# One inference step of a hybrid HGRN2 and attention layer on one core: VectorE's front tiles, the reciprocals' rings and the adaLN sums

## The chip, the core and the metric

The kernel runs on one core of one Trainium2 chip. The core has TensorE (PE, matmuls into PSUM), VectorE (DVE), ScalarE (ACT), GpSimd (POOL) and SyncE (SP, which here issues most DMAs). The engines run side by side, each through its own queue in order, and wait for each other on semaphores. The metric is the device time of one execution in microseconds, as a median over runs.

## What is computed

One trunk layer over 1024 latent tokens and 256 context tokens of width 1024, in float32:

```python
m = silu(cond) @ w_ada + b_ada                 # adaLN: 6 x 1024 columns, for c and c_ctx
sh1, sc1, g1, sh2, sc2, g2 = split(m, 6)
h = rms_norm(x, norm_mix_w) * (1.0 + sc1) + sh1
z = h @ w_in                                   # hq, hf (two directions), hi, hg, aq, ak, av, gl
o_a = attention(q, k, v)                       # 8 heads, 2 kv heads; latent: 512 cached + 1024 keys
o_h = rms_norm(hgrn(...)) * silu(hg)           # two directions, 4 heads, chunks of 32
g = sigmoid(gl)
merged = g[0] * (o_h @ w_ho) + g[1] * (o_a @ w_ao)
x = x + g1 * (merged @ w_out)
h = rms_norm(x, norm_ffn_w) * (1.0 + sc2) + sh2
x = x + g2 * (square(relu(h @ w_ff1)) @ w_ff2)
y = rms_norm(x, final_norm_w)
```

Context and latent tokens have conditioning vectors of their own, so each adaLN column is needed twice.

## The kernel before

**Numbers.** A matrix product is made of three matmuls in the format fp32r: each operand is split into a high part (rounded, written by ScalarE in `split`, L312) and a low part (the rest, a subtraction on VectorE, L313). L345, L346 and L347 are high x high, high x low and low x high in `mm3`; L362 to L364 the same with tokens as output rows.

**Tokens.** They come in three tiles, `TT`: t=0 and t=1 of 512 latent tokens, t=2 of 256 context tokens. Activations lie transposed, 128 channels by the tile's tokens, in eight chunks `kc`.

**Order.** TensorE's instructions run in the order in which the program issues them. The other engines' are put in order by the framework's scheduler ahead of time, with priorities from the program's order; `tc.high_priority` moves one up, and `tc.issue_after(x)` keeps one behind `x`. Tiles live in rings: `RINGS` gives the number of buffers of each, `RING_OF` the ring of each name. A tile that asks for a buffer waits until the last reader of an earlier tile is done. Ring X has 20 buffers, B 4, D 3, F and G 2. PSUM has two banks under the tag "t" (`ps_t`).

**The front.** The rows of x are loaded, normalised and transposed into `ps_t` (`norm1_tr`, L285). `norm1_col` then makes the modulated activation: ScalarE writes the high part `hi` from PSUM (L297); a full value `xn` is made from PSUM, by ScalarE (L302) or, for `kc` 1, 4 and 7 of t=0 and t=1, by VectorE (L300); VectorE subtracts, `lo = xn - hi` (L303). `front_z` uses both (L644, L645, L650).

**adaLN sums.** The first 16 of 48 column chunks (of 128) are made in the front. The others come in pairs of chunks, in two ways. `ada_sum` works on GpSimd: a 1024x256 block of `w_ada` is loaded into one of the two buffers of `wraw`, which the weights of `w_in` use too, multiplied by the conditioning vector and added over its eight row blocks (L197 to L204), for both vectors, into the two accumulators `ACC`. Its `late` lets TensorE add over the 128 partitions: four matmuls with the accumulator as the stationary operand and one column of ones as the moving one (L210), then VectorE adds the bias (L212). `ada_cols` does a whole pair on TensorE in four column groups (L178), evicts on ScalarE (L180), transposes (L184) and adds on VectorE.

**The filler.** While attention runs, `with_ada` yields the matmuls of ten groups of `w_in` columns (hq, hf, hf, hi, hg, twice); `Filler` feeds them in between attention's own, spread evenly. Groups of hi and hg are token-wise (`grp.tok`). In each group but the first there is one `ada_sum`: started at 0.25 of the group and finished at 0.9, in the last at 0.02 and 0.42; nine pairs in all. During the HGRN scans a second filler yields the gate logits' eight groups (`gls`), and seven pairs are made there by `ada_cols`.

**Attention's output.** `trans` transposes the exponentials into `ps_t` (L877), ScalarE and VectorE split them (L880), `value` multiplies by V (L891, L892). Sums of exponentials are turned into reciprocals and stored as rows in `RS`; outputs go to `OA`, those of HGRN to `OH`.

**The projections.** After the last gate logits, for t in the order 0, 2, 1, eight tiles `or` are loaded from `OH` (c < 4) and `OA`; for `OA` a second tile `or` of reciprocals is loaded, broadcast over 64 partitions each, and multiplied in (L1337); each is split into `oT` (L312, L313), in the buffers that `hT`, the activations of the gate logits, leave free. Then for each of eight output chunks and each t, `mm3` multiplies by `w_hgrn_out` and `w_attn_out`.

Of the kernel before, what the change touches and what calls it, by code (L numbers as in the profile page):

```python
# [11 lines left out]
AF = mybir.ActivationFunctionType  # L12
ALU = mybir.AluOpType
AX = mybir.AxisListType

P = 128
D = 1024
# [27 lines left out]
def build(ctx, tc, I, O, C):  # L45
# [15 lines left out]
    def close(*names):  # L61
        for n in names:
            open_pools.pop(n).close()
# [9 lines left out]
    def PS(tag, shape=(P, 512)):  # L73
        tag = "g" if tag == "p" else tag
        return ps.tile(list(shape), F32, tag=tag, name="ps_" + tag, bufs=PSB[tag])

    def S(shape=(P, 512), dt=F32, name=None, ring=None):
        ring = ring or RING_OF[name]
        return (xb if ring == "X" else sb if ring in "DE" else sl).tile(list(shape), dt, tag="s" + ring, name=name, bufs=RINGS[ring])
# [20 lines left out]
    def dma(out, in_):  # L100
        return sp.dma_start(out=f32(out), in_=f32(in_))
# [4 lines left out]
    def f32(ap):  # L106
        return ap.bitcast(F32)
# [85 lines left out]
    def ada_sum(ci, acc):  # L193

        raw = wraw(I["w_ada"], KC, ci * P)
        w = [ada_l[:, :, c:c + 1].broadcast_to([P, KC, 256]) for c in range(2)]
        g_.tensor_tensor(acc[0], raw[:, 0], w[0][:, 0], op=ALU.mult)  # L197
        for k in range(1, KC):
            g_.tensor_tensor(acc[1], raw[:, k], w[0][:, k], op=ALU.mult)
            g_.tensor_tensor(acc[0], acc[0], acc[1], op=ALU.add)  # L200
        g_.tensor_tensor(raw, raw, w[1], op=ALU.mult)
        for n in (4, 2):
            g_.tensor_tensor(raw[:, 0:n], raw[:, 0:n], raw[:, n:2 * n], op=ALU.add)
        g_.tensor_tensor(acc[1], raw[:, 0], raw[:, 1], op=ALU.add)  # L204

        def late():
            pt = PS("t")
            for b in range(2):
                for c in range(2):
                    pe.matmul(pt[:, 2 * c + b:2 * c + b + 1], acc[c][:, b * P:(b + 1) * P], ones, start=True, stop=True)  # L210
            with tc.high_priority(offset=600):
                v.tensor_tensor(modc[:, :, ci:ci + 2], pt[:, 0:4].rearrange("p (c b) -> p c b", c=2),  # L212
                                cols[:, B_ADA + ci:B_ADA + ci + 2].unsqueeze(1).broadcast_to([P, 2, 2]), op=ALU.add)
        return late


# [21 lines left out]
    def hpair(t):  # L238
        n = TT[t][1]
        if n == 512:  # L240
            return H(t), H(t)
        x = h_first.pop() if h_first else H(2)
        return x[:, 0, :], x[:, 1, :]
# [44 lines left out]
    def norm1_col(t, kc, pt, blocks=None):  # L288
        t0, n, cond = TT[t]
        if not blocks or blocks[0] == 0:  # L290
            hT[t][kc] = hpair(t)
        c = slice(blocks[0] * P, blocks[-1] * P + P) if blocks else slice(0, n)
        hi, lo = [x[:, c] for x in hT[t][kc]]
        pt, xn = pt[:, c], xnb[:, kc % 4, c]
        sc, sh = s1[:, cond, kc:kc + 1], modc[:, cond, kc:kc + 1]
        with tc.high_priority(offset=600):
            made = s_.activation(hi, pt, AF.Identity, scale=sc, bias=sh)  # L297

            if kc % 3 == 1 and t < 2:
                v.tensor_scalar(xn, pt, sc, sh, op0=ALU.mult, op1=ALU.add)  # L300
            else:
                s_.activation(xn, pt, AF.Identity, scale=sc, bias=sh)  # L302
            low[0] = v.tensor_tensor(lo, xn, f32(hi), op=ALU.subtract)  # L303
        return made

    low = [None]
# [938 lines left out]
    def zh(c):  # L1245
        return (Group(HQ + 256 * c, hq_consume(c), False), Group(HF + 256 * c, hf_consume(0, c), False),
                Group(HF + 512 + 256 * c, hf_consume(1, c), False), Group(HI + 256 * c, hi_consume(c), True),
                Group(HG + 256 * c, hg_consume(c), True))
# [3 lines left out]
    def with_ada(groups, ahead, behind):  # L1252

        late = []
        for i, grp in enumerate(groups):
            nxt = groups[i + 1] if i + 1 < len(groups) else None
            at, acts = 0.0, []
            if i and ahead:
                ci = ahead.pop(0)
                t0, t1 = (0.25, 0.9) if nxt else (0.02, 0.42)  # L1260
                acts = [(t0, lambda: late.append(ada_sum(ci, ACC))), (t1, lambda: late.pop()())]
            for need, n, gen in grp.stages():
                if not grp.tok and need == (0,):
                    jobs = [(0.5, lambda: grp.part(1))]
                elif nxt:
                    jobs = [(0.05, nxt.load), (0.5, lambda: nxt.part(0))]
                    if nxt.tok and not grp.tok:
                        jobs.append((0.75, lambda: nxt.part(1)))
                else:
                    jobs = []  # L1270
                for j, x in enumerate(gen):
                    if 0 in need and j == 6 and todo:
                        todo.pop()()
                    while jobs and j >= jobs[0][0] * n:
                        jobs.pop(0)[1]()
                    at += x
                    while acts and at >= acts[0][0] * 26.2:
                        acts.pop(0)[1]()
                    yield x
            if behind:  # L1280
                ci = behind.pop(0)
                todo.append(ada_cols(PS("g"), wraw(I["w_ada"], KC, ci * P), ci))
                yield 1.8
        if todo:
            todo.pop()()

    fz = Filler(with_ada([*zh(0), *zh(1)], list(range(16, 34, 2)), []), 250.0)
    while pending:
        fz.add(1.0)
        flush(1.0)  # L1290
# [4 lines left out]
    gls = [Group(GL + 256 * c, gl_consume(c), False) for c in range(8)]  # L1295
    with tc.high_priority(offset=600):
        gls[0].part(0)
    fg = Filler(with_ada(gls, [], list(range(34, 48, 2))), 196.0)
    hgrn(fg, fz.rest)
    fg.rest()  # L1300
    close("sl")
    wo1 = pool("wo1")

# [17 lines left out]
        return GR[r:r + 8, :].rearrange("(o a) b -> o (a b)", o=1).broadcast_to([P, D])  # L1321


    MT = (0, 2, 1)
    oT = [[None] * 8 for _ in range(3)]
    for t in MT:
        n = TT[t][1]
        for c in range(8):
            r = S(name="or")
            dma(r[:, 0:n], (OH if c < 4 else OA)[c % 4][t])  # L1330
            if c >= 4:
                q = S(name="or")
                for i in range(2):
                    r0 = 10 * (2 * (c - 4) + i) + TT[t][0] // P
                    row = RS[r0:r0 + n // P, :].rearrange("(o b) p -> o (b p)", o=1)
                    dma(q[64 * i:64 * i + 64, 0:n], row.broadcast_to([64, n]))
                v.tensor_tensor(r[:, 0:n], r[:, 0:n], q[:, 0:n], op=ALU.mult)  # L1337
            oT[t][c] = hpair(t)
            split(oT[t][c][0], oT[t][c][1], r[:, 0:n])
    mg = [[None] * KC for _ in range(3)]  # L1340
    WO = [[None] * 4 for _ in range(2)]

# [674 lines left out]
```

## Time and profile before

| what | value |
|---|---|
| median of 3 runs | 2041.67 us (2040.69 to 2041.69) |
| the profiled execution | 2040.07 us |
| its span, first to last instruction | 2038.3 us |
| mean granted TensorE clock | 0.999 |
| front, then the first products of attention | to about 131 us |
| attention, with the first filler | about 131 to 700 us |
| HGRN, with the second filler | about 700 to 1001 us |
| rest of the gate logits, then projections | to 1015 us, then from 1015 us |

The profile is one execution. A page gives the busy time of each engine, the chain of work that ended last and the costliest groups of instructions; further views give the instructions in order of time, the waits (who waited for whom) and the busy time of stretches. A line such as L313 can be a helper's and stand for many tiles: the names of the tiles (out<-in) tell them apart.

### The profile page before, as it was taken

The numbers are of one execution on the slowest core, as the hardware profiler recorded it, in microseconds if no ns is written. First come the engines' busy times: TensorE is split into PE (matmuls) and PEld (weight loads), VectorE is DVE, ScalarE is ACT, GpSimd is POOL, SyncE is SP. The second block draws the span as 40 slices with busy tenths as digits, with TensorE's granted clock in tenths as the row PEclk, the third lists the DMA queues.
The fourth block names the chain that finished last, engine by engine and source line by source line (L and its number), as shares of the span: only waits on it lengthen the run. The fifth ranks groups of instructions, "written<-read, shape, count | busy, mean of one in ns | idle before, by whom it ended". The sixth has DMA issues, their size and how long they took to land.

```text
span 2038.3 us, 33049 instructions
## 1 busy us (share of the span) xinstructions
PE 2004.0 (98%) x12246; PEld 1734.4 (85%) x12246; DVE 1346.3 (66%) x2474; ACT 940.0 (46%) x1965; POOL 526.7 (26%) x594
## 2 busy tenths in 40 slices
PE   7899999999999999999999999999999999999998
PEld 5698889988889988888878889988888888888886
DVE  5865665655665789877355635886666666577786
ACT  4635555555565423323312335755545544333443
POOL 1471321433303655544022101222112200000120
PEclk9999999999999999999999999999999999999999
DMA  9452211322122455554844424854454489455764
GB/s 317 155 193 83 81 58 47 105 93 76 38 92 80 149 158 175 160 176 149 249 145 143 170 104 148 258 183 146 146 164 145 147 309 357 135 166 171 237 236 138
DMA packets 222626, 320.00 MB, mean 157 GB/s; under 512 B 19161, under 2 KB 140801, under 8 KB 222465
## 3 DMA queue, kind: packets, MB, share of 16 engines
q1 hardware_dynamic: 209984, 277.99, 42.8%
q0 software_dynamic: 12480, 39.91, 5.3%
q8 instruction: 96, 1.57, 0.3%
q14 instruction: 66, 0.53, 0.1%
HBM read 232.05 MB, written 85.78 MB: 156 GB/s over the span
## 4 chain that ended last, share of the span: by engine, by line
PE 90%; DMA 4%; DVE 3%; ACT 1%; issue 1%; SPq 0%; POOL 0%; POOLq 0%; DVEq 0%; ACTq 0%
PE ps_g L345 8%; PE ps_g L346 7%; PE ps_g L347 7%; PE ps_s L845 4%; PE ps_t L877 4%; PE ps_g L362 2%; PE ps_g L892 2%; PE ps_g L364 2%; PE ps_g L363 2%; PE ps_g L1804 2%; PE ps_g L1806 2%; PE ps_g L1805 2%; PE ps_g L891 2%; PE ps_s L1649 2%; PE ps_s L1651 2%; PE ps_s L1650 2%
## 5 line engine op out<-in xcount | busy, mean ns | idle before, releaser
L345 PE MATMUL ps_g<-hs,wsp 128*128 128x512 f32 (+1 forms) x896 | 322.6, 360 | 0.0
L346 PE MATMUL ps_g<-hs,wsp 128*128 128x512 f32 (+1 forms) x896 | 309.2, 345 | 2.9 <-DVE hs L313 2.9
L347 PE MATMUL ps_g<-hs,wsp 128*128 128x512 f32 (+1 forms) x896 | 309.3, 345 | 0.0
L312 ACT ACTIVATE wsp<-wraw 128x512 fp32r<-128x512 f32 (+1 forms) x186 | 116.7, 668 | 208.4 <-PE ps_g L346 81.2
L846 DVE TENSOR_REDUCE mx<-ps_s 128x1 f32<-128x512 f32 (+1 forms) x208 | 138.1, 668 | 112.6 <-PE ps_s L845 110.6
L880 DVE TENSOR_TENSOR pTl<-ps_t,pTh 128x512 fp32r<-128x512 f32 x200 | 136.4, 684 | 88.0 <-ACT pTh L880 87.6
L313 DVE TENSOR_TENSOR wsp<-wraw,wsp 128x512 fp32r<-128x512 f32 (+1 forms) x186 | 147.4, 817 | 70.0 <-ACT wsp L312 69.7
L347 PEld LDWEIGHTS ps_g<-hs,wsp 128*128 128x128 f32 x896 | 169.3, 189 | 21.7
L345 PEld LDWEIGHTS ps_g<-hs,wsp 128*128 128x128 f32 x896 | 169.6, 189 | 20.3 <-issue 4.4
L346 PEld LDWEIGHTS ps_g<-hs,wsp 128*128 128x128 f32 x896 | 169.9, 190 | 18.2 <-DVE hs L313 3.4
L880 ACT ACTIVATE pTh<-ps_t 128x512 fp32r<-128x512 f32 x200 | 118.2, 602 | 139.3 <-PE ps_t L877 137.6
L312 ACT ACTIVATE ah<-ar 128x640 fp32r<-128x640 f32 (+1 forms) x112 | 80.9, 723 | 185.9 <-PE ps_g L1805 102.3
L857 ACT ACTIVATE pexp<-ps_s,ngm 128x512 f32<-128x512 f32 (+1 forms) x208 | 137.4, 669 | 42.7 <-DVE ngm L850 42.3
L313 DVE TENSOR_TENSOR ah<-ar,ah 128x640 fp32r<-128x640 f32 (+1 forms) x112 | 92.0, 822 | 78.2 <-ACT ah L312 77.8
L845 PE MATMUL ps_s<-Kl,Ql 128*128 128x512 f32 (+1 forms) x416 | 129.5, 411 | 0.0
L877 PE MATMUL ps_t<-ident,pexp 128*128 128x128 f32 x800 | 120.0, 272 | 0.1
L362 PE MATMUL ps_g<-wsp,hs 128*128 128x256 f32 x400 | 115.8, 289 | 0.0
L364 PE MATMUL ps_g<-wsp,hs 128*128 128x256 f32 x400 | 112.9, 282 | 0.0
L363 PE MATMUL ps_g<-wsp,hs 128*128 128x256 f32 x400 | 112.6, 281 | 0.0
L892 PE MATMUL ps_g<-pTl,Vl 128*128 128x256 f32 x400 | 104.2, 283 | 0.2
L891 PE MATMUL ps_g<-pTh,Vl 128*128 128x256 f32 x400 | 104.0, 281 | 0.0
L877 PEld LDWEIGHTS ps_t<-ident,pexp 128*128 128x128 f32 x800 | 94.4, 140 | 9.5 <-issue 0.6
(436 smaller groups left out, 5363.0 us busy)
## 6 DMA issues: line engine op xcount, KB each, us to landing
ar<-AF SPq DMA_DIRECT2D x112, 320.0 KB, 3.3
wraw<-in_w_ff SPq DMA_DIRECT2D x32, 1024.0 KB, 6.4
wr<-in_w_ff SPq DMA_DIRECT2D x128, 256.0 KB, 4.4
wraw<-in_w_in SPq DMA_DIRECT2D x18, 1024.0 KB, 5.6
wraw<-in_w_ada SPq DMA_DIRECT2D x16, 1024.0 KB, 5.4
AF<-a POOLq DMA_DIRECT2D x48, 256.0 KB, 2.7
AF<-t POOLq DMA_DIRECT2D x48, 256.0 KB, 2.3
wa<-in_w_ada SPq DMA_DIRECT2D x32, 256.0 KB, 5.9
```

The source lines that it names most:

```text
L312: s_.activation(hi, raw, AF.Copy)
L313: return v.tensor_tensor(lo, raw, f32(hi), op=ALU.subtract)
L345: pe.matmul(out, hi[:, k, :], mh, start=(first and k == 0), stop=False)
L346: pe.matmul(out, hi[:, k, :], ml, start=False, stop=False)
L347: pe.matmul(out, lo[:, k, :], mh, start=False, stop=(last and k == kcs - 1))
L362: pe.matmul(po[:, bb, :], mh[:, off:off + P], wh[:, k % 4, :], start=(k == 0), stop=False)
L363: pe.matmul(po[:, bb, :], mh[:, off:off + P], wl[:, k % 4, :], start=False, stop=False)
L364: pe.matmul(po[:, bb, :], ml[:, off:off + P], wh[:, k % 4, :], start=False, stop=(k == KC - 1))
L845: pe.matmul(pq[:, 0:n], self.qh[:, q0:q0 + P], K[self.g][var][self.kts[i]], start=(var == 0), stop=(var == 1))
L877: pe.transpose(pt[:, a, j * P:(j + 1) * P], self.Ps[j][i][:, b * P:(b + 1) * P], ident)
L880: behind[:] = s_.activation(hi, pt, AF.Copy), v.tensor_tensor(lo, pt, f32(hi), op=ALU.subtract)
L892: pe.matmul(pv[:, 0:256], V[self.g][kg][:, b, :], lo[:, a, :], start=False, stop=(k == last))
```

## The change

In the front, VectorE's pair for `kc` 1, 4, 7 is another: the product with the scale less the high part, from PSUM in one operation, and then the shift added, which gives the low part. The adaLN sums finish in another form: ones as the stationary operand, 32 columns wide, in four column groups, with the accumulator moving; ScalarE evicts, and a third step, `last`, transposes and adds the bias. In token-wise groups there are two sums (at 0.02 to 0.49 and 0.5 to 0.97), so that twelve pairs come from `ada_sum` and four from `ada_cols`. The loads for the projections stand ahead of `close("sl")`; the reciprocals (`rb`) take buffers in rings B, G, D and F, t=2's rows and reciprocals come in double tiles, and the order of products and splits is written out.

```diff
@@ ada_sum
         def late():
-            pt = PS("t")
-            for b in range(2):
-                for c in range(2):
-                    pe.matmul(pt[:, 2 * c + b:2 * c + b + 1], acc[c][:, b * P:(b + 1) * P], ones, start=True, stop=True)
-            with tc.high_priority(offset=600):
-                v.tensor_tensor(modc[:, :, ci:ci + 2], pt[:, 0:4].rearrange("p (c b) -> p c b", c=2),
-                                cols[:, B_ADA + ci:B_ADA + ci + 2].unsqueeze(1).broadcast_to([P, 2, 2]), op=ALU.add)
+            pa = PS("t")
+            for q in range(4):
+                pe.matmul(pa[32 * q:32 * q + 32, 0:P], ones.broadcast_to([P, 32]), acc[q // 2][:, (q % 2) * P:(q % 2 + 1) * P], start=True, stop=True)
+            ev = S((P, P), name="ev")
+            s_.activation(ev, pa[:, 0:P], AF.Copy)
+
+            def last():
+                pt = PS("t")
+                pe.transpose(pt[:, 0:P], ev, ident)
+                with tc.high_priority(offset=600):
+                    v.tensor_tensor(modc[:, :, ci:ci + 2], pt[:, 0:P].rearrange("p (c b x) -> p c b x", c=2, b=2)[:, :, :, 0],
+                                    cols[:, B_ADA + ci:B_ADA + ci + 2].unsqueeze(1).broadcast_to([P, 2, 2]), op=ALU.add)
+            return last
         return late
@@ norm1_col
             if kc % 3 == 1 and t < 2:
-                v.tensor_scalar(xn, pt, sc, sh, op0=ALU.mult, op1=ALU.add)
+                v.scalar_tensor_tensor(xn, pt, sc, f32(hi), op0=ALU.mult, op1=ALU.subtract)
+                low[0] = v.tensor_scalar(lo, xn, sh, None, op0=ALU.add)
             else:
                 s_.activation(xn, pt, AF.Identity, scale=sc, bias=sh)
-            low[0] = v.tensor_tensor(lo, xn, f32(hi), op=ALU.subtract)
+                low[0] = v.tensor_tensor(lo, xn, f32(hi), op=ALU.subtract)
@@ with_ada
             if i and ahead:
-                ci = ahead.pop(0)
-                t0, t1 = (0.25, 0.9) if nxt else (0.02, 0.42)
-                acts = [(t0, lambda: late.append(ada_sum(ci, ACC))), (t1, lambda: late.pop()())]
+                def begin():
+                    late.append(ada_sum(ahead.pop(0), ACC))
+
+                def end():
+                    late.append(late.pop()())
+                acts = [(0.02, begin), (0.45, end), (0.49, lambda: late.pop()())] if grp.tok else []
+                if nxt:
+                    acts += [(0.5 if grp.tok else 0.25, begin), (0.93, end), (0.97, lambda: late.pop()())]
@@ after with_ada
-    fz = Filler(with_ada([*zh(0), *zh(1)], list(range(16, 34, 2)), []), 250.0)
+    fz = Filler(with_ada([*zh(0), *zh(1)], list(range(16, 40, 2)), []), 250.0)
...
-    fg = Filler(with_ada(gls, [], list(range(34, 48, 2))), 196.0)
+    fg = Filler(with_ada(gls, [], list(range(40, 48, 2))), 190.0)
     hgrn(fg, fz.rest)
     fg.rest()
+
+    MT = (0, 2, 1)
+    oT = [[None] * 8 for _ in range(3)]
+
+    rows_a, first = {}, last_split[0]
+    for t in MT:
+        t0, n, cond = TT[t]
+        for c in range(0, 8, 1 if t < 2 else 2):
+            w = 1 if t < 2 else 2
+            x = S((P, w, n), name="or")
+            for j in range(w):
+                dma(x[:, j], (OH if c < 4 else OA)[c % 4 + j][t])
+                rows_a[t, c + j] = x[:, j]
+            if c < 4:
+                continue
+            q = S((P, w, n), name="rb", ring=("B", "G" if c < 6 else "D", "F")[t])
+            for i in range(2):
+                rows = RS.rearrange("(c i b) p -> c i b p", c=4, i=2)[c - 4:c - 4 + w, i, t0 // P:(t0 + n) // P]
+                dma(q[64 * i:64 * i + 64], rows.rearrange("(o c) b p -> o c (b p)", o=1).broadcast_to([64, w, n]))
+            with tc.issue_after(first.ins):
+                v.tensor_tensor(x, x, q, op=ALU.mult)
+        if t == 1:
+            break
+        for c in range(8):
+            oT[t][c] = hpair(t)
+            parted = split(oT[t][c][0], oT[t][c][1], rows_a[t, c])
+        if t == 0:
+            first = parted
+    for c in range(8):
+        oT[1][c] = hpair(1)
+        with tc.issue_after(parted.ins):
+            split(oT[1][c][0], oT[1][c][1], rows_a[1, c])
     close("sl")
     wo1 = pool("wo1")
...
-    MT = (0, 2, 1)
-    oT = [[None] * 8 for _ in range(3)]
-    for t in MT:
-        n = TT[t][1]
-        for c in range(8):
-            r = S(name="or")
-            dma(r[:, 0:n], (OH if c < 4 else OA)[c % 4][t])
-            if c >= 4:
-                q = S(name="or")
-                for i in range(2):
-                    r0 = 10 * (2 * (c - 4) + i) + TT[t][0] // P
-                    row = RS[r0:r0 + n // P, :].rearrange("(o b) p -> o (b p)", o=1)
-                    dma(q[64 * i:64 * i + 64, 0:n], row.broadcast_to([64, n]))
-                v.tensor_tensor(r[:, 0:n], r[:, 0:n], q[:, 0:n], op=ALU.mult)
-            oT[t][c] = hpair(t)
-            split(oT[t][c][0], oT[t][c][1], r[:, 0:n])
```

## The prediction

> **What bounds the kernel now.** I read the page first: busy shares and the chain that ended last.
>
> ```profile
> span 2038.3 us, 33049 instructions
> PE 2004.0 (98%) x12246; PEld 1734.4 (85%) x12246; DVE 1346.3 (66%) x2474; ACT 940.0 (46%) x1965; POOL 526.7 (26%) x594
> PE 90%; DMA 4%; DVE 3%; ACT 1%; issue 1%; SPq 0%; POOL 0%; POOLq 0%; DVEq 0%; ACTq 0%
> ```
>
> TensorE is the bound: 98% busy, 90% of the chain. So an edit counts for the TensorE time it removes or adds, plus the waits of TensorE that it ends or makes. Outside its work are 34 us (2038.3 less 2004.0), start and end included; the waits have names in the view of waits, asked for TensorE alone:
>
> ```profile
> PE ps_t L285 <- ACT xnb L302: 4.0, 4, 1.4
> PE ps_g L346 <- DVE hs L313: 2.9, 2, 2.1
> ...
> PE ps_s L346 <- DVE hs L313: 0.9, 1, 0.9
> ...
> PE ps_t L285 <- DVE xnb L300: 0.8, 1, 0.8
> ...
> PE ps_t L210 <- DVE pTl L880: 0.7, 2, 0.4
> PE ps_t L285 <- DVE kT L313: 0.5, 1, 0.5
> PE ps_g L650 <- DVE hs L303: 0.4, 1, 0.4
> ```
>
> Columns: who waited for whom, us in total, times, longest. The change touches three of these places: the front (L285, L650), the adaLN sums (L210), and the start of the branch projections (L346 waiting for a split's low part, 3.8 us).
>
> **Part 1, front tiles.** For kc 1, 4, 7 of t 0 and 1, VectorE's pair changes: a tensor_scalar from PSUM and a two-input subtract become a scalar_tensor_tensor from PSUM and a tensor_scalar in SBUF. Groups by line and form, then two single lines:
>
> ```profile
> L303 DVE TENSOR_TENSOR hs<-xnb,hs 128x512 fp32r<-128x512 f32 x14 | 9.6, 689 | 3.6 <-ACT xnb L302 3.6
> L300 DVE TENSOR_SCALAR xnb<-ps_t,s,modc 128x512 f32<-128x512 f32 x5 | 4.0, 806 | 0.9 <-ACT hs L297 0.9
> L279 DVE TENSOR_SCALAR xr<-xr,rst x20: 478/481/488, 9.6 to 65.4; 128x512 f32<-128x512 f32 x20
> L1372 DVE SCALAR_TENSOR_TENSOR gt<-gt,ps_s x24: 409/676/691, 1026.9 to 1131.4; 128x512 f32<-128x512 f32 x16, 128x256 f32<-128x256 f32 x8
> ```
>
> Before, a wide pair is 806 + 689 = 1495 ns. After, by the nearest rows of the same forms, 676 (L1372, one operand in PSUM) + 481 (L279, one SBUF source) = 1157. That is 0.34 us for each of five wide pairs, and about half for each of the two narrow ones: VectorE saves some 2.0 us. TensorE gains only where VectorE was the last to be ready: 0.8 + 0.5 + 0.4 = 1.7 us; the 4.0 us are ScalarE's, whose two operations per tile stay. The first operation now needs ScalarE's high part. That adds no wait of weight: the row of L300 shows it already starting behind that instruction (0.9 us of idle time, ended by hs L297). I take **-0.5 us**, a third of the 1.7, because most of these waits also have an ACT operation close behind. Bounds: -1.7, and +0.5 if the queue falls out in another order.
>
> **Part 2, adaLN sums.** One old finish on TensorE, and one sum done wholly on TensorE (L178, then its transpose L184), from the timeline:
>
> ```profile
> 660.41 0.28 PE L364 MATMUL ps_g<-wsp,hs 128*128 128x256 f32 x1
> 660.53 0.28 PE L210 MATMUL ps_t<-ones,sums 128*128 128x1 f32 x2
> ...
> 661.34 0.37 PE L845 MATMUL ps_s<-Kl,Ql 128*128 128x256 f32 x1
> ```
>
> ```profile
> 986.03 0.28 PE L347 MATMUL ps_g<-hs,wsp 128*128 128x256 f32 x1
> 986.24 1.08 PE L178 MATMUL ps_g<-wraw,ada_l 128*32 128x128 f32 x32
> 987.25 0.50 PE L345 MATMUL ps_g<-hs,wsp 128*128 128x512 f32 x1
> ...
> 992.19 0.27 PE L184 MATMUL ps_g<-ident,ev 128*128 128x128 f32 x1
> 992.22 0.47 PE L345 MATMUL ps_g<-hs,wsp 128*128 128x512 f32 x1
> 992.53 0.39 PE L346 MATMUL ps_g<-hs,wsp 128*128 128x512 f32 x1
> ```
>
> The old finish holds TensorE from 660.53 to 661.34: 0.81 us for 8 instructions. Nine of them are 7.3 us. The TensorE sum holds it from 986.15 (L347's start and the 0.12 us between such matmuls) to 987.25: 1.10 us, of which 32 x 0.026 = 0.83 are the instructions and 0.27 the entry and exit; its transpose adds 0.03 and a next matmul 0.08 longer (0.31 for the usual 0.23): 1.21 together. Three such sums go over to GpSimd: 3.6 us. The new finish is 8 instructions in L178's form (8 x 0.026 = 0.21), the same 0.27, and a transpose like L184 (0.11): 0.59 us, twelve times 7.1. Net: 7.1 - 7.3 - 3.6 = -3.8 us.
>
> The Trainium skill, TensorEngine Tiling (Array Packing), Key Properties, says that changing the tiling mode drains TensorE, which speaks against twelve short visits to the four-column-group form. The trace agrees with something of the kind: 0.27 us around 32 instructions. If entry and exit cost the doubled 0.54, the net would be -0.6 us in place of -3.8.
>
> New waits: a finish now takes two ps_t banks in turn, in a ring of two that attention's transposes share. Before, nine takings cost 0.7 us of waiting for pTl (the L210 row above); 24 at the same rate cost 1.9, so +1.2. ScalarE gets twelve evictions of 128x128, which cost nothing as long as one is ready when the transpose comes, 0.04 of a group later. A group lasts some 63 us here (the first finish at 217.2, the eighth at 660.53, seven groups on), so there are 2.5 us of cover:
>
> ```profile
> L180 ACT ACTIVATE ev<-ps_g x7: 259/268/273, 741.8 to 987.6; 128x128 f32<-128x128 f32 x7
> L857 ACT ACTIVATE pexp<-ps_s,ngm 128x512 f32<-128x512 f32 (+1 forms) x208 | 137.4, 669 | 42.7 <-DVE ngm L850 42.3
> L210 PE MATMUL ps_t<-ones,sums x36: 164/250/250, 217.2 to 683.7; 128*128 128x1 f32 x36
> ```
>
> 0.27 behind one exponential of 0.67 fits. GpSimd has to finish a sum between one finish (which frees the accumulators) and the next, now 0.43 to 0.5 of a group in the token-wise groups, 27 us at least until the last:
>
> ```profile
> POOL sums L197 <- PE ps_t L210: 177.0, 5, 56.9
> 141.00:161.20 20.20, 20.20 (x112) 17.38 (x111) 6.04 (x10) 4.81 (x9) 18.69 (x19) 1.00 0.50 173
> 661.30:682.60 21.30, 21.30 (x182) 21.30 (x182) 12.94 (x31) 11.50 (x31) 19.91 (x20) 1.00 0.39 127
> ```
>
> The windows' sixth figure is POOL's busy time: 18.7 us for a sum, 19.9 with one gate multiplication in between. The 177 us show GpSimd idle until a finish frees the accumulators, with weights already there. So 20 us go into 27, and the last sum into the same 22 us that the last one has now (660.53 to 683.25). Part 2: -3.8 + 1.2 = **-2.6 us**; bounds -4.5 (no wait left) and the rivals below.
>
> **Part 3, reciprocals in other rings.** TensorE and then VectorE at the start of the projections:
>
> ```profile
> 1015.12 0.40 PE L345 MATMUL ps_s<-hs,wsp 128*128 128x512 f32 x1
> ...
> 1020.59 0.28 PE L345 MATMUL ps_s<-hs,wsp 128*128 128x256 f32 x1
> ...
> 1022.33 0.39 PE L346 MATMUL ps_s<-hs,wsp 128*128 128x256 f32 x1 [0.92 <-DVE hs L313]
> ...
> 1025.21 0.39 PE L346 MATMUL ps_g<-hs,wsp 128*128 128x256 f32 x1 [0.82 <-DVE hs L313]
> ...
> 1027.95 0.39 PE L346 MATMUL ps_g<-hs,wsp 128*128 128x256 f32 x1 [2.12 <-DVE hs L313]
> ```
>
> ```profile
> 1005.63 7.30 DVE L313 TENSOR_TENSOR hs<-or,hs 128x512 fp32r<-128x512 f32 x12
> 1019.31 0.69 DVE L1337 TENSOR_TENSOR or<-or 128x512 f32<-128x512 f32 x1 [6.37 <-DMA or<-RS]
> ...
> 1027.47 1.02 DVE L313 TENSOR_TENSOR hs<-or,hs 128x256 fp32r<-128x256 f32 x2
> ```
>
> TensorE idled 0.92 + 0.82 + 2.12 = 3.9 us. The low parts of t=2 that TensorE wanted at 1021 to 1026 came as late as 1027 to 1028, because VectorE, in order, stood 6.4 us for reciprocals of t=1 and did t=1's products between them. These loads were late because rows and reciprocals, 24 + 12 tiles, share a ring of 20. After, the rows need exactly 20 tiles (8 + 4 + 8) and the reciprocals have rings of their own; the order is fixed as t=0, t=2, t=1. VectorE's twelve splits of 7.30 us give 0.61 each. The high and low parts of t=2 can be written once TensorE has left the gate logits at 1015.1; 8 narrow ones at 0.5 (1.02 for two) are done by 1019, ahead of 1020.59; t=1's eight take 4.9 more, to 1024, while TensorE is on t=2 until about 1026.2, less the first half wanted at 1023.5, when six are ready. Twelve multiplications become ten, before 1015. Loads: 48 DMAs become 44. t=1's four reciprocals have two buffers, so the third load on SyncE waits for the first product, and what is queued behind it there (stores of gate logits, projection weights) waits as long; TensorE has no wait for any of these among its waits above. I take **-3.8 us**; bounds -3.9 and 0, and +2 if that queue bites.
>
> **Sum.** -0.5 - 2.6 - 3.8 = -6.9 us. The profiled execution took 2040.07 us, 1.8 more than its span; it would take 2033.2. It is 1.6 below the median shown; the forecast for the median is 2041.67 - 6.9 = **2034.8 us**, 0.34% faster. About 0.2% (4.1 us) is what a measurement of this kernel tells from no change.
>
> **Rivals.**
> (a) The projections' wait does not go: VectorE's order brings t=2 late again, or its loads queue up on SyncE. For it: one in-order queue feeds both. Against: the count of tiles. Without the 3.8: -3.1, 2038.6.
> (b) GpSimd is late for the last sum. Its weights need a buffer of a ring of two; if they get not the earlier sum's but that of the group's own weights, free here only at 666.46, they land 5.5 us on:
>
> ```profile
> 666.46 0.39 SPq L101 DMA_DIRECT2D wraw<-in_w_in  x1
> DMA to landing us min/median/max: 5.1/5.5/6.7
> L200 POOL TENSOR_TENSOR sums<-sums,pvt x63: 728/742/1061, 142.7 to 672.3; 128x256 f32<-128x256 f32 x63
> ```
>
> then 21 us of GpSimd end at 693, against a finish at some 684.5: 8.5 us, the total +1.6, 2043.3. Against it: SyncE issued such loads as early as a buffer allowed. The Trainium skill, SBUF — State Buffer, section SBUF: two separate sides, has GpSimd and VectorE lock a shared port pair against each other; L200's spread (742, at most 1061) agrees, and three more sums meet more of it.
> (c) Slower: the eviction misses its transpose. ScalarE's queue is in order; if the eviction stands there behind an exponential that waits for its maximum, TensorE, in order too, waits in each of twelve sums. With the 2.5 us of cover used up and 1.6 us more (two exponentials of 0.67 and 0.27), 12 x 1.6 = 19.2: the total +12.3, 2054.0. Slower than now from 0.6 us a sum on, by over 0.2% from 0.92 on.
> (d) It does not do what it says: the four column groups don't overlap with one matmul each, so that 8 take 0.81 as now; 12 x 0.60 = +7.2, the total +0.3, 2042.0. L178's 32 in 0.83 speaks against it.
>
> **Chances.** Forecast 0.59 (2031 to 2037.5), (a) 0.15, (b) 0.12, (c) 0.09, (d) 0.05. Faster than 2037.6: 0.59; slower than 2045.8: (c), 0.09; within: 0.32. The range runs from 2030.5 (the lower bounds, -1.7 - 4.5 - 3.9 = -10.1, and 1.0 for the runs' own spread) to 2042.5, which takes in (a), (d) and nearly half of (b).
>
> **What would show it.** Right: L346 no longer waiting around 1022 to 1028; the new column-group matmuls 8 in about 0.2 us; four L178 runs for seven; the first of the pair near 0.68 and the second near 0.48. Wrong: TensorE waiting at the new transpose for ev, at the column sums for GpSimd's accumulators, or at L346 for another tile's split.

## The result, and the profile after

The changed kernel takes **2037.69 us** (median of 21 runs, 2035.18 to 2040.07) where the kernel before takes 2042.36 on the same chip (21 runs, 2039.58 to 2044.98): ratio 0.9977 [0.9970, 0.9984], 4.7 us or 0.23% faster. The forecast was 6.9 us faster, a median of 2034.8; 2037.69 lies inside its range (2030.5 to 2042.5) and just outside the 2031 to 2037.5 that it held the likeliest. That the sum came out near is in part luck, since its terms did not come near: the front, put at -0.5, lost 3 to 5 us; the rings and projections, put at -3.8, gained 5 to 6; the sums, put at -2.6, gained 3 to 4.

First the page of the changed kernel: span, busy shares, and the chain that ended last.

```profile
span 2035.3 us, 32988 instructions
PE 2000.8 (98%) x12183; PEld 1728.6 (85%) x12183; DVE 1347.4 (66%) x2469; ACT 942.6 (46%) x1974; POOL 584.3 (29%) x651
PE 92%; DMA 3%; DVE 2%; ACT 1%; issue 1%; SPq 0%; POOL 0%; POOLq 0%; DVEq 0%; ACTq 0%
```

TensorE is still the bound. It has 3.2 us less work (2000.8 for 2004.0), and its idle time has not moved: 34.5 us (2035.3 less 2000.8) for 34.3. VectorE should have saved 2 us in the front and is 1.1 us busier, GpSimd has its three sums more. So waits went at one place and came at another. Their names, from the view of TensorE's waits (who waited for whom: us in total, times, longest):

```profile
PE ps_t L291 <- DVE qT L320: 3.5, 2, 3.2
PE ps_t L291 <- ACT xnb L309: 2.9, 3, 1.4
PE ps_t L291 <- DVE xnb L306: 2.1, 2, 1.4
PE ps_s L1677 <- DVE a L1711: 1.2, 1, 1.2
PE ps_g L657 <- DVE hs L310: 0.7, 1, 0.7
```

The 3.8 us for split low parts at the start of the projections are gone. The transpositions of the front (L291) waited 5.6 us in all before (the three rows shown there and 0.3 for qT) and wait 8.5 now, 3.2 of it in one piece for qT.

Cutting both profiles at the same TensorE instructions gives the table that the rest of this document uses (us, changed less before, from one profile each; the other columns are the experiments below).

| stage | changed | e1 | e2 | e3 | e4 | e5 | e10 | e12 |
|---|---|---|---|---|---|---|---|---|
| front, to the transposition of t=1's kc 7 | -0.15 | -0.21 | -0.16 | +0.60 | +0.26 | +0.27 | +0.28 | +0.37 |
| front, from there to t=2's kc 3 | **+2.87** | -0.02 | +2.86 | -0.02 | 0.00 | -0.01 | 0.00 | +1.04 |
| front, from there to AQ's first matmul | +1.57 | -0.04 | -0.01 | -0.04 | -0.01 | -0.02 | -0.01 | -0.04 |
| attention | +0.41 | +0.12 | -0.04 | +0.13 | -0.01 | -0.24 | +3.01 | +0.28 |
| HGRN and the other gate logits | -3.88 | -3.88 | -0.73 | -3.90 | -0.87 | -0.75 | -3.90 | -3.88 |
| projections | **-4.81** | -4.81 | +4.36 | +1.12 | -4.59 | +1.79 | -4.81 | -4.81 |
| out-projection and first feed-forward product | +1.07 | +0.15 | +0.05 | +0.60 | +0.71 | -0.05 | +4.87 | +1.17 |
| the rest | -0.13 | -0.36 | -1.23 | -0.47 | -0.13 | +0.80 | +0.44 | +1.02 |
| span | -3.05 | -9.04 | +5.10 | -1.98 | -4.64 | +1.79 | -0.12 | -4.86 |

Of the HGRN row, 0.8 us is a wait for GpSimd (`usf`, no part of the change) that the profile of before has and none of the others: e2, e4 and e5, which leave that stage as it was, come out 0.7 to 0.9 shorter as well.

### The front, read closely

Only the second and third front rows differ. Here are the waits of TensorE there, from its timeline, before and then after (start, length, work, and in brackets the idle time ahead of it and who ended it):

```profile
67.51 0.66 PE L285 MATMUL ps_t<-ident,xr 128*128 128x128 f32 x4 [0.84 <-DVE xnb L300]
78.60 0.44 PE L285 MATMUL ps_t<-ident,xr 128*128 128x128 f32 x2 [0.50 <-DVE kT L313]
80.15 0.44 PE L285 MATMUL ps_t<-ident,xr 128*128 128x128 f32 x2 [1.11 <-ACT xnb L302]
```

```profile
67.37 0.66 PE L291 MATMUL ps_t<-ident,xr 128*128 128x128 f32 x4 [0.70 <-DVE xnb L306]
75.79 0.44 PE L291 MATMUL ps_t<-ident,xr 128*128 128x128 f32 x2 [1.35 <-DVE xnb L306]
82.87 0.44 PE L291 MATMUL ps_t<-ident,xr 128*128 128x128 f32 x2 [3.22 <-DVE qT L320]
```

The last row of each is the same transposition, kc 3 of t=2. Before, it waited 1.11 us for ScalarE's `xnb`: it was written into the `ps_t` bank of the transposition just ahead of it. After, it waits 3.22 us for the low part of q: it was given the bank in which q's transposes lie. VectorE's timeline, before and then after, shows that q itself is no later (L320 is the subtraction that makes q's low part, L313 before):

```profile
73.27 0.41 DVE L494 TENSOR_TENSOR qa<-qa,qb 128x256 f32<-128x256 f32 x1
73.60 0.80 DVE L300 TENSOR_SCALAR xnb<-ps_t,s,modc 128x512 f32<-128x512 f32 x1
74.32 1.10 DVE L490 TENSOR_TENSOR qa<-qn,cosb 128x512 f32<-128x512 f32 x1
...
80.61 1.79 DVE L490 TENSOR_TENSOR qa<-qn,cosb 128x512 f32<-128x512 f32 x1
82.32 0.68 DVE L313 TENSOR_TENSOR qT<-ps_t,qT 128x512 fp32r<-128x512 f32 x1
```

```profile
72.36 1.52 DVE L501 TENSOR_TENSOR qa<-qa,qb 128x256 f32<-128x256 f32 x1
73.80 0.67 DVE L485 TENSOR_REDUCE qss<-sq 128x8 f32<-128x512 f32 x1
74.40 0.67 DVE L497 TENSOR_TENSOR qa<-qn,cosb 128x512 f32<-128x512 f32 x1
75.00 0.74 DVE L306 SCALAR_TENSOR_TENSOR xnb<-ps_t,s,hs 128x512 f32<-128x512 f32 x1
...
82.14 0.68 DVE L320 TENSOR_TENSOR qT<-ps_t,qT 128x512 fp32r<-128x512 f32 x1
```

q's low part is done at 83.00 before and at 82.82 after. Before, nobody on TensorE needed its bank by then. The other new wait, 1.35 us, is for the first operation of the new pair, kc 7 of t=1: it runs at 75.00 for 73.60. Some 0.6 us of that is L497, the rotation's multiplication, which now stands ahead of it in VectorE's queue and stood behind it before (as L490); the other 0.8 is that the operations ahead of both end later, at 74.47 for 73.68. Each operation of the pair is as quick as forecast or nearly (the view of one line, after: count, shortest/median/longest ns):

```profile
L306 DVE SCALAR_TENSOR_TENSOR xnb<-ps_t,s,hs x7: 477/743/751, 20.7 to 75.0; 128x512 f32<-128x512 f32 x5, 128x256 f32<-128x256 f32 x2
L307 DVE TENSOR_SCALAR hs<-xnb,modc x7: 353/476/487, 21.9 to 77.1; 128x512 fp32r<-128x512 f32 x5, 128x256 fp32r<-128x256 f32 x2
```

So the theory to test, **"bank"**: the pair is not slow; with it the framework's scheduler lays out VectorE's order and the two `ps_t` banks differently, and the new layout makes TensorE wait. (Whether the scheduler answers to the pair's shorter time or to its new need of ScalarE's high part is not separated by any run.) Its rivals: **"series"** or **"pair"**, each new pair holds its bank longer because its first operation needs ScalarE's high part, and **"queue"**, only the later place of kc 7's product counts.

The third row, +1.57, has another cause. The windows of the changed kernel (the stretch, its us, then the busy time and count of PE, PEld, DVE, ACT and POOL, the granted clock, the DMA share and GB/s):

```profile
83.00:87.00 4.00, 4.00 (x12) 3.16 (x13) 1.36 (x2) 1.02 (x2) 0.66 (x1) 0.57 0.19 66
87.00:91.00 4.00, 4.00 (x22) 3.29 (x21) 0.85 (x2) 2.10 (x6) 0.00 (x0) 1.00 0.19 66
```

Right behind the long wait the clock is 0.57 for 4 us, and TensorE does 12 matmuls in the time of 22. The last section returns to this.

### The profile page after: what moved, and what is told of

It reads as the page before. It is cut to its first block, busy times and chain, and to the rows that moved or that the text cites. A ratio compares the mean times of both kernels' runs of the same rounds, so it can differ in the third digit from the quotient of the medians.

```text
span 2035.3 us, 32988 instructions
## 1 busy us (share of the span) xinstructions
PE 2000.8 (98%) x12183; PEld 1728.6 (85%) x12183; DVE 1347.4 (66%) x2469; ACT 942.6 (46%) x1974; POOL 584.3 (29%) x651
## 3 DMA queue, kind: packets, MB, share of 16 engines
q8 instruction: 96, 1.57, 0.3%
## 4 chain that ended last, share of the span: by engine, by line
PE 92%; DMA 3%; DVE 2%; ACT 1%; issue 1%; SPq 0%; POOL 0%; POOLq 0%; DVEq 0%; ACTq 0%
PE ps_g L352 8%; PE ps_g L354 8%; PE ps_g L353 8%; PE ps_s L852 5%; PE ps_t L884 4%; PE ps_g L369 2%; PE ps_g L899 2%; PE ps_g L371 2%; PE ps_g L898 2%; PE ps_g L370 2%; PE ps_g L1832 2%; PE ps_g L1834 2%; PE ps_g L1833 2%; PE ps_s L1677 2%; PE ps_s L1678 2%; PE ps_s L1679 2%
## 5 line engine op out<-in xcount | busy, mean ns | idle before, releaser
L320 DVE TENSOR_TENSOR wsp<-wraw,wsp 128x512 fp32r<-128x512 f32 (+1 forms) x186 | 152.9, 845 | 86.7 <-ACT wsp L319 86.5
L320 DVE TENSOR_TENSOR ah<-ar,ah 128x640 fp32r<-128x640 f32 (+1 forms) x112 | 92.0, 822 | 76.8 <-ACT ah L319 75.8
L852 PE MATMUL ps_s<-Kl,Ql 128*128 128x512 f32 (+1 forms) x416 | 130.0, 412 | 0.0
L369 PE MATMUL ps_g<-wsp,hs 128*128 128x256 f32 x400 | 116.6, 291 | 0.0
L371 PE MATMUL ps_g<-wsp,hs 128*128 128x256 f32 x400 | 112.9, 282 | 0.0
L164 POOL TENSOR_TENSOR frst<-ms,mexp 128x1 f32<-128x1 f32 x10 | 11.5, 1153 | 320.8 <-DVE ssf L1921 278.1
```

The costliest lines, as they stand in the source:

```text
L320: return v.tensor_tensor(lo, raw, f32(hi), op=ALU.subtract)
L369: pe.matmul(po[:, bb, :], mh[:, off:off + P], wh[:, k % 4, :], start=(k == 0), stop=False)
L371: pe.matmul(po[:, bb, :], ml[:, off:off + P], wh[:, k % 4, :], start=False, stop=(k == KC - 1))
L852: pe.matmul(pq[:, 0:n], self.qh[:, q0:q0 + P], K[self.g][var][self.kts[i]], start=(var == 0), stop=(var == 1))
```

## The experiments

All were timed in five rounds beside the kernel before.

### Undoing the pair, and doing it alone

e1 is the changed kernel with the old pair, e2 the kernel before with the new one.

```diff
-                v.scalar_tensor_tensor(xn, pt, sc, f32(hi), op0=ALU.mult, op1=ALU.subtract)
-                low[0] = v.tensor_scalar(lo, xn, sh, None, op0=ALU.add)
+                v.tensor_scalar(xn, pt, sc, sh, op0=ALU.mult, op1=ALU.add)
             else:
                 s_.activation(xn, pt, AF.Identity, scale=sc, bias=sh)
-                low[0] = v.tensor_tensor(lo, xn, f32(hi), op=ALU.subtract)
+            low[0] = v.tensor_tensor(lo, xn, f32(hi), op=ALU.subtract)
```

> The changed kernel with VectorE's old pair of operations in the front (a full value from PSUM, then the subtraction); sums and rings stay changed. Theory A (the new pair itself, by what it does to the front's order, costs the front 4.2 us): the front is as before, TensorE's point at 92 us comes at 92, and the total is 4.2 us below the changed kernel, about 8.9 us below before (ratio to before 0.9957). Theory C (the front's loss comes with the sums or the rings, whose instructions shift the scheduler's plan): the front keeps its loss, and the ratio stays 0.9977.

> The kernel before with the new pair alone. Theory A: +4.2 us, ratio 1.002, with TensorE waiting some 3 us for qT's low part between 79 and 83 us and for kc 7's product before that. Theory C: no change, ratio 1.000. The prediction's own step (-0.5 us): 0.9998.

e1: 2031.77 us, ratio **0.9958** [0.9945, 0.9972], the front back to the kernel before. e2: 2045.38 us, ratio 1.0023 [1.0014, 1.0033]: the pair alone makes the kernel slower. The same 2.86 us stand in the same stretch of the front. Its other loss, 4.36 us in the projections, stands at waits that the kernel before has too (3.9 us in both), with a lowered clock behind them here (0.50 for 10 us). So the total of e2 is not the front's loss alone.

### Sums alone, rings alone

e3 is the kernel before with the second part of the change alone (`ada_sum`, `with_ada` and the two lists of the fillers in the diff above), e4 with the third alone (the block moved ahead of `close("sl")`).

> The kernel before with the changed adaLN sums alone. The prediction's step: -2.6 us (-3.6 in the HGRN stage, +1.0 in attention), ratio 0.9987. By the trace of the changed kernel: -3.9 in HGRN and +0.4 in attention, -3.5, ratio 0.9983. A rival, that the sums' gain needs the projections' new order: 0 to -1, with the wait of L346 longer than the 3.9 us of before.

> The kernel before with the reciprocals' rings and the written order alone. The prediction's step: -3.8 us, ratio 0.9981; by the trace of the changed kernel -4.8, 0.9976, with no wait of L346 left around 1022 to 1028 us. Rival (the wait went since there are fewer TensorE sums in HGRN's last third, which leaves VectorE and SyncE free earlier): half of it or less, above 0.999.

e3: 2036.99 us, 0.9981 [0.9972, 0.9989], -3.9 us. e4: 2035.29 us, 0.9971 [0.9960, 0.9982], -5.9 us. By these ratios the three parts alone add up to +4.7 - 3.9 - 5.9 = -5.1, and the whole change gives -4.7: no interplay shows, though each part is known to some 2 us only. In e4 no wait of the projections is left; the windows of that stage, in the kernel before and in the changed kernel, show what it was worth:

```profile
1015.10:1130.30 115.20, 111.34 (x579) 95.34 (x578) 62.75 (x95) 28.05 (x52) 29.93 (x24) 1.00 0.47 147
```

```profile
1015.90:1126.40 110.50, 110.50 (x580) 95.19 (x580) 62.06 (x91) 27.95 (x50) 30.63 (x24) 1.00 0.42 136
```

3.86 us of idle time, as forecast, and 0.84 us of busy time besides. In the timeline of before, the matmul behind each of the three waits takes 0.39 us in place of 0.28, and the one ahead of it counts for its whole 0.28 us, where the next would begin after 0.12; by these figures an estimate is 3 x (0.11 + 0.16) = 0.81.

### Which tiles of the front

e7 has the new pair for t=0 alone, e8 for t=1 alone, e9 for all but kc 7 of t=1; the others have the old pair.

```diff
-            if kc % 3 == 1 and t < 2:
+            if kc % 3 == 1 and t < 1:      # e7; e8: t == 1; e9: t < 2 and (t, kc) != (1, 7)
...
```

> The changed kernel with the new VectorE pair for t=0 alone; t=1 has the old pair. Here both the PSUM banks of the q transposes and the order on VectorE around kc 7 of t=1 fall out as before. Theory 'bank' (the front's loss comes from the q transposition that takes the bank for which the next x transposition has to wait): no loss, front within 0.5 us of the kernel before, total about 2031.8, ratio 0.9955. Rival 'queue' (the loss comes from kc 7 of t=1 standing two places later on VectorE): the same, no loss. Rival 'pair' (every new pair costs TensorE something, wherever it is): half of the tiles, so +2.1 in the front, about 2034, ratio 0.9967.

> The changed kernel with the new pair for t=1 alone. Banks and VectorE's order fall out as in the changed kernel. 'bank' and 'queue': the whole loss, front +4.3 us against the kernel before, total 2036 to 2037.7, ratio 0.9975. 'pair': half of it, +2.1, about 2034, ratio 0.9967.

> The changed kernel with the old pair for the one tile kc 7 of t=1 alone. VectorE's order is that of the changed kernel (the product two places later), but the q transposition takes the bank that it had before. 'bank': the 3.2 us wait for qT's low part goes, and with the product still late about 1.4 us of waiting stay: front +1 to +2, total about 2033.5, ratio 0.9963. 'queue': the whole loss, +4.3, ratio 0.9975. 'pair': five of six tiles, +3.6, ratio 0.9973.

e7: 2033.06 us, 0.9952 [0.9939, 0.9966]; e8: 2038.07 us, 0.9979 [0.9970, 0.9988]; e9: 2037.17 us, 0.9972 [0.9961, 0.9983]. In the stretch of the front they show 0.00, +2.87 and +2.94 us. Three new pairs cost nothing in e7 and as much as six in e8, so "pair" and "series" fall. e9 went against my reading of the banks. Its timeline has both waits in full, and the first is now for the old operation:

```profile
77.44 0.44 PE L291 MATMUL ps_t<-ident,xr 128*128 128x128 f32 x2 [1.42 <-DVE xnb L310]
84.52 0.44 PE L291 MATMUL ps_t<-ident,xr 128*128 128x128 f32 x2 [3.24 <-DVE qT L323]
```

I had taken it that the bank which q takes decides. By the expectation q has its old bank in e9 (the traces name no banks), and the loss is whole: what decides is the bank that kc 3 of t=2, the second transposition *behind* q, gets, and that is q's here too. e9 doesn't separate "bank" from "queue", since both are as in the changed kernel. The next two do.

### Taking the bank away from q

e11 makes q's transposes due later in the program's own plan of the front; e12 leaves the plan and writes kc 3 of t=2 into the tile of kc 2, by hand.

```diff
-    DUE = (3.4, 4.4, 10.0)
+    DUE = (3.4, 5.4, 10.0)      # e11 alone
...
-            made = norm1_col(t, kc, norm1_tr(t, rows_n[t], kc))
+            pt_k = norm1_tr(t, rows_n[t], kc, pt_k if (t, kc) == (2, 3) else None)
+            made = norm1_col(t, kc, pt_k)      # e12 alone
```

> The changed kernel, new pair everywhere, with the q transposes due 1 us later in the planner (5.4 for 4.4). VectorE's order around kc 7 of t=1 is that of the changed kernel; the q transposes come one step later and no x transposition has to wait for a bank that holds q right behind them. 'bank': the 3.2 us wait goes, front 0 to +1.5, total 2032 to 2034, ratio 0.9957 to 0.9967. 'queue' and 'pair': the loss stays, front about +4.3, ratio 0.9975. The later due time shifts the plan of what follows as well, worth up to a microsecond either way.

> The changed kernel with one thing fixed by hand: the transposition of kc 3 of t=2 is written into the same PSUM tile as that of kc 2 just before it, as it falls out in the kernel before, in place of the bank that q's transposes hold. Pair, VectorE's order and due times as in the changed kernel. 'bank': the 3.2 us wait for qT's low part goes, a wait of about 1.1 us for ScalarE's xnb comes in its place, and the 1.35 us wait behind VectorE's later product stays: front about +2.2 us against the kernel before (+4.3 in the changed kernel), total about 2035.5, ratio 0.9967. Rival 'VectorE is late': the k transposition further on takes q's bank now and waits there as long; front +4.3, ratio 0.9977.

e12: **2033.58 us, 0.9959** [0.9946, 0.9971], with the new pair everywhere. Its timeline:

```profile
76.31 0.44 PE L291 MATMUL ps_t<-ident,xr 128*128 128x128 f32 x2 [1.36 <-DVE xnb L306]
81.55 0.44 PE L291 MATMUL ps_t<-ident,xr 128*128 128x128 f32 x2 [1.38 <-ACT xnb L309]
```

The wait for the product behind VectorE's later place is still there (1.36), the one for q is gone, and 1.38 for ScalarE's `xnb` stands in its place: the stretch costs +1.04 where it cost +2.87, and no slow clock follows. The k transposition further on (84.57) does not wait for q either, as the rival "VectorE is late" would have it. So "bank" has 1.8 us of the 2.9, and "queue" the other 1.0. The ratio of the whole kernel moved further than that, from 0.9977 to 0.9959 (3.7 us); the slow clock's 1.57 us, which e12's profile doesn't have, would make most of the difference.

e11: 2044.10 us, 1.0011 [1.0002, 1.0020], slower than before. The front did what "bank" expects: 1.35 stays, no wait for q, -1.01 in the stretch and +0.37 behind it. But 13 us were lost behind the front. With q due later more of the filler's matmuls stand ahead of attention's first (57 groups of three where there were 38), and attention then waited for exponentials and for keys (2.5 and 1.6 us at L852), and 2.5 at L209 for a bank; the clock was halved twice, for 3.4 us each time. I had put that side effect at 1 us, and didn't follow it further.

### The form of a sum's finish

e10 is e1 with the old finish for all twelve sums; e5 is the kernel before with the new finish for its nine, at the old places, the transposition 0.04 of a group behind.

```diff
...
-                acts = [(0.02, begin), (0.45, end), (0.49, lambda: late.pop()())] if grp.tok else []
+                acts = [(0.02, begin), (0.45, end)] if grp.tok else []      # e10
...
-                acts = [(t0, lambda: late.append(ada_sum(ci, ACC))), (t1, lambda: late.pop()())]
+                acts = [(t0, lambda: late.append(ada_sum(ci, ACC))), (t1, lambda: late.append(late.pop()())), (t1 + 0.04, lambda: late.pop()())]      # e5
```

> The changed kernel with the old VectorE pair (the fastest so far, 2031.8, ratio 0.9958) and the old finish of the adaLN sums, still twelve of them on GpSimd and four on TensorE. Theory 'form pays': an old finish costs some 1.0 us of TensorE (0.81, 0.08 on the next matmul, 0.12 of waiting), a new one 0.77 (both from the attention stages measured so far), so three more sums in the old form make attention +3.0 us against the kernel before; HGRN -3.9, projections -4.8; total 2034.8, ratio 0.9973. With the terms of the forecast (0.81 and 0.59 and two waits each for a bank): about 2031.8 + 2.6 - 1.2 = 2033.2, ratio 0.9965. Theory 'count alone' (the form is worth nothing, only the three sums that leave TensorE): attention as in the changed kernel, 2031.8, ratio 0.9958.

> The kernel before with the new finish alone: still nine sums on GpSimd and seven on TensorE, at the old places, with the transposition 0.04 of a group behind the column sums. 'form pays': nine times 0.24 less, attention -2.2 us, everything else within 0.5; about 2039.5 where the kernel before takes 2041.7, ratio 0.9989. With the forecast's terms: 9 x (0.59 - 0.81) + 9/12 x 1.2 = -1.1, ratio 0.9995. 'count alone': 0, ratio 1.0. Should the sums wait at the transposition for the eviction, attention is longer: +1 to +2.

e10: 2038.56 us, 0.9983 [0.9974, 0.9992]. Attention is +3.01, the figure of "form pays", and so 2.9 longer than in e1. That it fits is in part luck: 12 x 0.16 = 1.9 are for the form, by the prices below (0.81 and 0.65), and 0.7 for a wait for GpSimd, shown below, that the theory didn't have. The total missed by 3.8 us: the stage with the first feed-forward product lost 4.87, a wait of 2.88 us for VectorE and a slow clock behind it. e5: 2041.04 us, 0.9995 [0.9987, 1.0004], no difference that can be told, attention -0.24 where "form pays" wants -2.2. The views of waits in attention say why. First the changed kernel, then e5:

```profile
PE ps_t L884 <- DVE pTl L887: 0.2, 1, 0.2
```

```profile
PE ps_t L883 <- DVE modc L217: 0.9, 3, 0.4
PE ps_t L209 <- DVE pTl L886: 0.7, 2, 0.4
PE ps_t L883 <- ACT ev L211: 0.5, 1, 0.5
PE ps_t L883 <- DVE pTl L886: 0.4, 1, 0.4
```

In e5 TensorE's busy time in attention, from about 157 us on, fell by 1.9 us (541.77 for 543.67), and its waits at the two `ps_t` banks rose from 0.7 to 2.5. The new form does cost less; whether it also costs bank waits hangs on where in a group it is put. At the places of the change it costs next to none (0.2 us in all).

## Why the prediction was right and wrong

**The bound.** Right: TensorE at 98%, and only its work and waits counted.

**Front, -0.5: wrong in sign.** The durations came out (0.74 for 0.68, 0.476 for 0.48), and "that adds no wait of weight" held for ScalarE's high part. The step that failed is the bound: "+0.5 if the queue falls out in another order". The stretch cost 2.9 us, 4.4 with the slow clock, all of it gone in e1. e2's total of +4.7 holds the projections' slow clock as well; its front, without a slow clock, lost 2.7. I counted what the saved time could win at each wait, and took the order around it as given. The price of another order stood in the trace of before: q's low part ends at 83.00, the transposition that could meet its bank starts at 80.15, so a change of bank costs up to 2.85. Two banks and a scheduler that puts VectorE's queue in order ahead of time were in the text; I didn't put them together.

**Sums, -2.6: right in mechanism, too small (-3.9 alone, 2.2 to 5.7 by its interval), with two terms off in opposite directions.** The three sums that leave TensorE: HGRN's busy time fell 3.4 us, forecast 3.6 (the windows of that stage, before and after):

```profile
702.00:1015.10 313.10, 312.31 (x2530) 266.42 (x2529) 240.30 (x563) 100.81 (x252) 142.51 (x152) 1.00 0.56 176
```

```profile
706.70:1015.90 309.20, 308.93 (x2431) 263.72 (x2430) 239.01 (x558) 100.50 (x252) 140.60 (x152) 1.00 0.55 174
```

The finish, priced at 0.59, from TensorE's timeline of the changed kernel:

```profile
640.87 0.28 PE L371 MATMUL ps_g<-wsp,hs 128*128 128x256 f32 x1
641.08 0.30 PE L209 MATMUL ps_t<-sums,ones 128*32 128x128 f32 x2
...
641.22 0.28 PE L209 MATMUL ps_t<-pvt,ones 128*32 128x128 f32 x2
641.43 0.39 PE L369 MATMUL ps_g<-wsp,hs 128*128 128x256 f32 x1
641.65 0.28 PE L370 MATMUL ps_g<-wsp,hs 128*128 128x256 f32 x1
```

A matmul of 128x256 gives way to the next after 0.12 us. The finish starts 0.21 behind L371 (0.09 more), lasts 0.35 to L369, and L369 holds 0.10 longer than usual: 0.54, with the transposition's 0.11 from the forecast 0.65. Around the eight instructions (0.21) are 0.33 us, for the 0.27 taken from L178; the doubled 0.54 that the prediction weighed didn't come. The waits, put at +1.2, did not come: 0.7 before, 0.2 after. The 0.7 for two of nine finishes is no rate: a finish waits or not by its place among attention's transposes, and the places were moved.

**Rings, -3.8: right in mechanism, too small.** No split is waited for; the profile gives -4.8, the runs of e4 -5.9 (3.7 to 8.2 by its interval). Missing were the 0.84 us of busy time around the waits. For the rest there are two candidates, which no run separates: the 0.8 us wait for `usf` that the profile of before has in the HGRN stage, and the slow clock that follows such waits in some executions (over all runs the mean granted clock is 0.9986 in e4 and 0.9972 in the kernel before beside it, about 2.9 us of 2040).

**Rivals.** (a), the projections' wait stays: no. (b), GpSimd late for the last sum: its weights did take the earlier sum's buffer, and it was just in time:

```profile
688.97 0.74 POOL L204 TENSOR_TENSOR pvt<-wraw 128x256 f32<-128x256 f32 x1
```

```profile
689.50 0.41 PE L209 MATMUL ps_t<-sums,ones 128*32 128x128 f32 x4
689.76 0.41 PE L209 MATMUL ps_t<-pvt,ones 128*32 128x128 f32 x4
```

The second accumulator is ready at 689.71, and its four column sums come 0.26 behind the first four in place of 0.01. In e10 TensorE waits there, by its view of waits:

```profile
PE ps_t L210 <- POOL pvt L204: 0.7, 1, 0.7
```

(c), the eviction misses its transposition: no wait at any of the twelve. (d), the column groups don't overlap: eight take 0.35 us with their exit, above.

**The +1.07 behind the projections** was not in the forecast. It holds a wait of TensorE for VectorE's `a` (L1677, 1.2 us) that the kernel before doesn't have; in nine of the eleven experiments that wait lasts 0.2 to 2.9 us, in e2 and e5 it doesn't come, in code that none of them touches. That it is the plan again is likely, and not shown.

## What to carry to other kernels

Where a scheduler lays out queues and buffers ahead of time, a changed operation is also another plan: before pricing the time it saves, look in the trace for the rings with few banks, see who holds each when the next user comes, and take "the next user gets the worst bank" as the bound. If the layout turns out bad, fix the bank by hand and keep the operation (e12, 0.9959), or leave the operation as it was (everywhere in e1, 0.9958, or in t=1 alone in e7, 0.9952; the three can't be told apart). And time the parts of a change alone: here one part took back half of what the other two gave.

## What the runs showed of the hardware

**Behind a wait of TensorE the clock can be low for some microseconds.** Slow stretches like the one at 83 us show up behind waits in other places: behind 2.88 us in e10, 1.52 in e3, 2.11 in e5, and in e2 behind 1.28 and 0.93. No run sets such a wait to a chosen length, so this is what the traces have side by side, and no threshold is shown. The windows of e10, with a slow stretch, and of e9, where the clock stays at 1.00 behind the 3.24 us wait:

```profile
1355.30:1359.30 4.00, 3.94 (x11) 3.13 (x12) 2.19 (x4) 3.10 (x5) 0.56 (x1) 0.60 0.64 218
```

```profile
84.70:88.70 4.00, 4.00 (x22) 3.32 (x21) 1.63 (x3) 1.74 (x4) 0.61 (x1) 1.00 0.19 66
```

For some 3.4 us matmuls take 0.63 us in place of 0.39, which costs about 1.6 us (the third front row); in e2 the clock is 0.50 for 10 us. It doesn't follow each time: the same 3.2 us wait in the front was followed by it in the changed kernel and in e8 (0.74 and 0.83 in two windows), not in e2 and e9, and the projections' waits of 1.07, 0.83 and 2.11 us in e5, not the same waits in the kernel before. The Trainium skill, TensorE: Matmul & The Clock Gate, in the section HAM oscillation, warns of gaps above about 3.4 us, after which the clock is halved; and says in Part 1 that the monitor's window runs freely. That fits a stretch that follows the same wait in one execution and not in another. But here slow stretches came behind gaps of 1.5 us, with shorter ones just ahead.

**VectorE beside GpSimd.** The rotation's 128x256 addition took 1.52 us at 72.36, where other operations of that size take 0.41. It ended at 73.88, 0.28 us behind GpSimd's multiplication that began at 71.91:

```profile
71.91 1.69 POOL L500 TENSOR_TENSOR qb<-qn,sinb 128x512 f32<-128x512 f32 x1 [1.03 <-DVE ms L163]
```

It stands ahead of kc 7's product there. In the kernel before another one, L490 at 80.61, took 1.79 us, where 0.68 is usual for its size, with a GpSimd multiplication from 80.43 to 81.85 beside it. That GpSimd is the cause is not tested here.
